# Small matmuls of the recurrence issued as groups with a higher rank, and modulation weights taken two blocks per step, in a two-layer hybrid backbone

## The chip, the cores and the metric

One core of one Trainium2 chip runs the whole program in a single launch. The metric is the device time of one execution in microseconds. The kernel before was run three times: 2420.04, 2423.49 and 2425.33 us, a median of 2423.49 us.

## The reference, cut to what matters

Two layers of one trunk run over 256 latent tokens and 256 context tokens of width 1024. A layer modulates a normalised input, projects it with one wide matrix into three token mixers, merges them, and then runs a feed-forward part: dense in layer 0, eight experts with two per token in layer 1.

```python
for i in range(DEPTH):
    mod = (silu_c @ w_mod[i] + b_mod[i])[:, None, :]      # 1024 -> 6144, for the latent row
    mod_c = silu_ctx @ w_mod[i] + b_mod[i]                # the same weights, for the context row
    ul = modulate(h, norm_mix[i], sh1, sc1) @ w_in[i]
    uc = modulate(hc, norm_mix[i], csh1, csc1) @ w_in[i]
    ...
def rwkv7_scan(S0, r, w, k, v, kk, a):                    # 8 heads, 2 directions, a 64x64 state
    S = S * w_t + (S @ -kk_t) (kk_t * a_t) + v_t k_t      # token by token
    y_t = S @ r_t
```

Two pieces of this are touched by the change. One is the modulation, a product of two vectors (latent and context) with a 1024x6144 matrix per layer. The other is the RWKV-7 recurrence, which the kernel computes in chunks of 64 tokens.

## The kernel before, in words

All operands are fp32. A large projection is done as three products of rounded halves (`mm3`, L917, L918 and L919): the weights arrive by DMA in a buffer `wraw`, ScalarE makes the rounded half `whi` (L893), VectorE makes the rest `wlo` (L895), and TensorE issues three matmuls of 128 rows by 128 columns of the array, mostly with 512 streamed columns. These are called large matmuls below. They use the array as one piece.

Four kinds of small matmuls use a part of the array, so that several can stand in it side by side:

- **Modulation** (`mods`, L1031). A block of 128 rows of the modulation matrix is streamed (128 columns, or 256 in the dense feed-forward stage of layer 0) against 32 columns of weights that hold the two vectors. Four such matmuls, one for each quarter `j` of the array's columns, belong to one block `k`; eight blocks are accumulated. `mods` is a generator that yields after each block. `fill` (MODF at L718) takes steps of it during the recurrence, `modnorm` (L1111) during the first norm, and `ffn` (L1470) two steps for each of 18 of its 22 column tiles, for the next layer.
- **Chunk products** (`rwkv_prod`, L389): 64 rows by 128 columns, 128 or 64 streamed columns; for each of four chunks one matmul for each of the two heads `h`, in two PSUM tiles `px`.
- **Inverse of a triangular block** (`rwkv_inverse`, L564, L573, L592, L602): 32 rows by 32 columns, 32 streamed columns; 32 matmuls (L564, L573) or 16 (L592, L602) in a row in the source.
- **Outputs of a chunk chain** (`rwkv_chain`, L658, L662): 128 rows by 64 columns.

The recurrence has eight units per layer (four head pairs, two directions). `rwkv_run` weaves the chain of one unit, the products and inverse of the next one, the elementwise part of the one after that, and `fill`, which supplies steps of the modulation and then of the large projections that other mixers need (`spills`). Weaving fixes only the order in which the source is traced. Each traced instruction gets a rank that counts up; when the program is built, a list scheduler keeps for each engine those instructions whose inputs and buffers its own model holds ready, and takes the one with the lowest rank. So each engine gets a fixed order of instructions before anything runs, and the hardware follows it.

PSUM has eight banks, dealt out by tag: the products use `aa` (two banks), the chain `ch` (one), the inverse `iv` (one), the outputs `oo` (one), modulation and spilled projections `fl` (two). `wraw` has four buffers.

Of the kernel before, what the change touches and what calls it, by code (L numbers as in the profile page):

```python
# [131 lines left out]
class Kern:  # L132
# [13 lines left out]


# [225 lines left out]
    def rwkv_prod(s, U):  # L373
# [7 lines left out]
        for half in range(2):  # L381
# [4 lines left out]
            for cc in range(4):  # L386
                c = half * 4 + cc
                for h, hr in enumerate(HRS):
                    nc.tensor.matmul(px[h][:, cc * 128:cc * 128 + N], U.BK[hr, c].rearrange("p a b -> p (a b)"), U.LA[hr, c].rearrange("p a b -> p (a b)")[:, 0:N], start=True, stop=True)  # L389
# [115 lines left out]
    def rwkv_inverse(s, Ac, FT):  # L505
# [55 lines left out]
        for u in range(8):  # L561
            for qd in range(4):
                qr = slice(qd * 32, qd * 32 + 32)
                nc.tensor.matmul(pq[qr, u * 32:u * 32 + 32], F16[qr, u, :], E[qr, u, :], start=True, stop=True)  # L564
# [5 lines left out]
        for u in range(8):  # L570
            for qd in range(4):
                qr = slice(qd * 32, qd * 32 + 32)
                nc.tensor.matmul(pe[qr, u * 32:u * 32 + 32], ET[qr, u, :], Q[qr, u, :], start=True, stop=True)  # L573
# [15 lines left out]
        for u in range(8):  # L589
            for h in range(2):  # L590
                a, b = slice(h * 64, h * 64 + 32), slice(h * 64 + 32, h * 64 + 64)
                nc.tensor.matmul(p2[b, u * 32:u * 32 + 32], FT[a, u, :], E2[a, u, :], start=True, stop=True)  # L592
# [6 lines left out]
        for u in range(8):  # L599
            for h in range(2):  # L600
                a, b = slice(h * 64, h * 64 + 32), slice(h * 64 + 32, h * 64 + 64)
                nc.tensor.matmul(pg[a, u * 32:u * 32 + 32], Q2[b, u, :], E2T[b, u, :], start=True, stop=True)  # L602
# [6 lines left out]
    def rwkv_chain(s, U):  # L609
# [12 lines left out]
        for k, c in enumerate(order):  # L622
# [27 lines left out]
            if c >= c0o and k % 4 == 3:  # L650

                po = s.tile(s.ps, [128, 512], "oo")
                g = c // 4
                for j in (g * 4, g * 4 + 2):
                    cb = j % 4 * 64
                    for odd, hr in enumerate(HRS):
                        if j + odd != order[0]:
                            mm(po[hr, cb:cb + 128], LA[:, j + odd, 1, :], S[:, order.index(j + odd) - 1], start=True, stop=False)  # L658
                    for h in range(2):
                        for odd, hr in enumerate(HRS):  # L660
                            first = j + odd == order[0]
                            mm(po[hr, cb + h * 64:cb + h * 64 + 64], MX[:, j + odd, h, 64:128], UV[:, j + odd, hs[h]], start=first, stop=first or h == 1)  # L662
# [55 lines left out]
MODF = [19, 10]  # L718
# [129 lines left out]
class Full(Kern):  # L848
# [162 lines left out]
    def mods(s, l):  # L1011
# [5 lines left out]
        for b in range(3):  # L1017
# [5 lines left out]
            for q in range(0, 4, n):  # L1023
                ps = s.tile(s.ps, [128, 512], s.mtag)
                for k in range(8):
                    if (b, q, k) in s.early:
                        wm = s.early.pop((b, q, k))
                    else:
                        wm = s.mod_block(l, b, q, k, s.wp, n)
                    for j in range(4):  # L1030
                        nc.tensor.matmul(ps[j * 32:j * 32 + 32, 0:n * 128].rearrange("p (q x) -> p q x", q=n), s.S[:, k, :], wm[:, :, j], start=k == 0, stop=k == 7)  # L1031
                    yield
# [70 lines left out]
    def modnorm(s, pool, gain, ish, isc, tts, mods=None):  # L1103
# [359 lines left out]
    def ffn(s, pool):  # L1463
# [5 lines left out]
        for f in range(22):  # L1469
            s.step(s.gen, 2 if f < 18 else 0)  # L1470
# [319 lines left out]
    def run(s, out):  # L1790
# [40 lines left out]
        s.step(s.gen, 4)  # L1831
# [112 lines left out]
```

## Time and profile before

| what | value |
|---|---|
| median of 3 runs | 2423.49 us |
| the profiled execution's own time | 2412.98 us |
| span of the profile, first to last instruction | 2411.2 us |
| mean granted TensorE clock, as a share | 0.97 |
| TensorE (PE) busy, and its matmul records | 2262.6 us, 15772 |
| weight loads (PEld) busy | 1785.6 us |
| VectorE (DVE) busy | 1538.5 us |
| ScalarE (ACT) busy | 1170.4 us |

A matmul on plain fp32 operands leaves two records in the trace, so a single small matmul reads as x2 and a group of 32 as x64; a large matmul leaves one. The start of a record is measured, its end is modelled. Matmuls overlap in the array, so what one costs is read from the distance between starts, not from its length. Some 1290 us of the span hold small matmuls of the four kinds above: the norm and recurrence of layer 0 (about 10 to 614 us), the dense feed-forward part (about 822 to 1135 us) and the norm and recurrence of layer 1 (about 1286 to 1659 us).

### The profile page before, as it was taken

To read this page: it belongs to the slowest core of one execution; us is meant where nothing else is said; L and a number is where in the kernel's file an instruction comes from. 1 tells how busy PE (TensorE), PEld (TensorE's weight loads), DVE (VectorE), ACT (ScalarE), POOL (GpSimd) and SP (SyncE) were. 2 spreads that over 40 slices of the span, in tenths; PEclk is the share of its full clock that TensorE was granted. 3 is DMA by queue.
4 is the path that set the end of the run, shared out by engine and by line. 5 is a ranking of instruction groups with operands and counts; after the bars stand their busy time and mean duration, and the time that the engine had idled before them with its cause. 6 is when DMAs were issued, how large, how long until landed. Compare 5 with 4: busy or idle time off the path is not lost. (4 is left out here: it accounts for less than half of the span.)

```text
span 2411.2 us, 41643 instructions
## 1 busy us (share of the span) xinstructions
PE 2262.6 (94%) x15772; PEld 1785.6 (74%) x15772; DVE 1538.5 (64%) x2994; ACT 1170.4 (49%) x2150; POOL 355.6 (15%) x307
## 2 busy tenths in 40 slices
PE   7989999999999989999998999999998989999996
PEld 4767777787667767778876777878867768878775
DVE  5776666655566453333227678777567578888897
ACT  4544444544543342222226554565363457777765
POOL 1311112101002210000013221130111211111120
PEclk9999999999999999999999999999899989999998
DMA  7343432223235424443223333322325658988895
GB/s 259 110 141 127 139 122 71 76 87 117 94 113 157 160 81 162 169 162 104 95 79 124 111 113 117 115 65 91 114 71 162 216 174 320 336 306 318 309 319 192
DMA packets 160609, 373.69 MB, mean 155 GB/s; under 512 B 18016, under 2 KB 35424, under 8 KB 160400
## 3 DMA queue, kind: packets, MB, share of 16 engines
q1 hardware_dynamic: 160400, 370.94, 45.9%
q8 instruction: 126, 2.06, 0.4%
q14 instruction: 83, 0.68, 0.1%
HBM read 345.18 MB, written 25.69 MB: 154 GB/s over the span
## 5 line engine op out<-in xcount | busy, mean ns | idle before, releaser
L895 DVE TENSOR_TENSOR wlo<-wraw,whi 128x512 fp32r<-128x512 f32 (+4 forms) x666 | 652.6, 1001 | 347.9 <-ACT whi L893 334.7
L893 ACT CAST whi<-wraw 128x512 fp32r<-128x512 f32 (+4 forms) x666 | 536.8, 820 | 557.2 <-PE mm L918 226.6
L917 PE MATMUL fl<-xh,whi 128*128 128x512 f32 (+1 forms) x816 | 317.0, 389 | 2.8 <-ACT whi L893 2.7
L919 PE MATMUL fl<-xh,wlo 128*128 128x512 f32 (+1 forms) x816 | 306.7, 376 | 6.7 <-DVE wlo L895 6.5
L918 PE MATMUL fl<-xl,whi 128*128 128x512 f32 (+1 forms) x816 | 302.4, 371 | 0.0
L919 PEld LDWEIGHTS fl<-xh,wlo 128*128 128x128 f32 x816 | 157.7, 193 | 31.6 <-DVE wlo L895 10.0
L917 PEld LDWEIGHTS fl<-xh,whi 128*128 128x128 f32 x816 | 158.0, 194 | 27.9 <-issue 6.0
L918 PEld LDWEIGHTS fl<-xl,whi 128*128 128x128 f32 x816 | 158.2, 194 | 21.3 <-issue 4.7
L917 PE MATMUL mm<-xh,whi 128*128 128x512 f32 (+1 forms) x416 | 165.6, 400 | 2.0 <-ACT pad L1797 1.0
L919 PE MATMUL mm<-xh,wlo 128*128 128x512 f32 (+1 forms) x416 | 162.5, 391 | 3.2 <-DVE wlo L895 3.1
L918 PE MATMUL mm<-xl,whi 128*128 128x512 f32 (+1 forms) x416 | 163.5, 393 | 0.0
L918 PE MATMUL mm<-wlo,xgh 128*128 128x512 f32 (+1 forms) x384 | 146.5, 381 | 15.3 <-DVE wlo L895 14.8
L917 PE MATMUL mm<-whi,xgh 128*128 128x512 f32 (+1 forms) x384 | 144.3, 378 | 0.2 <-ACT xs L1665 0.2
L919 PE MATMUL mm<-whi,xgl 128*128 128x512 f32 (+1 forms) x384 | 143.7, 374 | 0.0
L1696 POOL TENSOR_TENSOR H<-H,yt 128x512 f32<-128x512 f32 x29 | 56.1, 1960 | 392.5 <-DVE yt L1695 392.5
L918 PEld LDWEIGHTS mm<-wlo,xgh 128*128 128x128 f32 x384 | 72.2, 188 | 37.0 <-DVE wlo L895 27.0
L917 PEld LDWEIGHTS mm<-xh,whi 128*128 128x128 f32 x416 | 78.3, 189 | 27.3 <-ACT whi L893 4.9
L919 PEld LDWEIGHTS mm<-xh,wlo 128*128 128x128 f32 x416 | 78.4, 188 | 20.9 <-DVE wlo L895 4.9
L636 PEld LDWEIGHTS ch<-Pb,TT 128*128 128x128 f32 x512 | 71.8, 194 | 26.2 <-DVE Pb L630 17.3
L918 PEld LDWEIGHTS mm<-xl,whi 128*128 128x128 f32 x416 | 78.6, 189 | 16.3 <-DVE xl L711 0.8
L646 DVE SCALAR_TENSOR_TENSOR Sd<-ch,e2c,Se 64x64 f32<-64x64 f32 x192 | 53.8, 280 | 56.0 <-PE ch L641 53.4
L636 PE MATMUL ch<-Pb,TT 128*128 128x64 f32 x512 | 79.3, 278 | 8.9 <-DVE Pb L630 8.1
(527 smaller groups left out, 4688.1 us busy)
## 6 DMA issues: line engine op xcount, KB each, us to landing
wraw<-in_ws_dram SPq DMA_DIRECT2D x284, 512.0 KB
wraw<-in_ws_dram SPq DMA_DIRECT2D x302, 256.0 KB
wraw<-in_w_mod_dram SPq DMA_DIRECT2D x96, 256.0 KB
wraw<-in_ws_dram SPq DMA_DIRECT2D x64, 384.0 KB
wraw<-in_w_mod_dram SPq DMA_DIRECT2D x32, 512.0 KB
wm<-in_w_mod_dram SPq DMA_DIRECT2D x32, 256.0 KB
spg<-stg SPq DMA_DIRECT2D x24, 256.0 KB
mth<-spg SPq DMA_DIRECT2D x24, 256.0 KB
```

What stands on the lines that cost most here:

```text
L636: mm(ch[:, 128 + h * 64:192 + h * 64], U.TF[:, (2 * c + h) * 64:(2 * c + h) * 64 + 128], Pb[:, hs[h]], start=True, stop=True)
L646: nc.vector.scalar_tensor_tensor(S[hr, k, hr], ch[hr, o], e2c[hr, c, :], Se[hr, hr], ALU.mult, ALU.add)
L893: s.nc.scalar.copy(hi, raw)
L895: s.follow(s.nc.vector.tensor_sub(lo, raw, hi.bitcast(F32)))
L917: mm(out, ah, bh, start=start, stop=False)
L918: mm(out, ah, bl, start=False, stop=False)
L919: mm(out, al, bh, start=False, stop=stop)
L1696: eng.tensor_tensor(s.h[2 + i][:, ns], s.h[2 + i][:, ns], t, ALU.add)
```

## The change

A context `together` lowers the rank of each instruction traced inside it by 60, so that it competes with instructions that were traced 60 places earlier. It is put around the matmul loops of the chunk products, of the four steps of the inverse, of the chain's outputs, and of the modulation. In the modulation two blocks are taken per step, and the step counts are halved: MODF from 19 and 10 to 10 and 5, 3 and 5 steps in place of 5 and 9 in the first norm, one step for each of 20 column tiles in `ffn` in place of two for each of 18. The same matmuls, DMAs and vector instructions are issued as before, in another order.

```diff
+    def together(s):
+
+        return s.tc.high_priority(60)
...
             px = [s.tile(s.ps, [128, 512], "aa") for _ in HRS]
-            for cc in range(4):
-                c = half * 4 + cc
-                for h, hr in enumerate(HRS):
-                    nc.tensor.matmul(px[h][:, cc * 128:cc * 128 + N], ...
+            with s.together():
+                for cc in range(4):
+                    c = half * 4 + cc
+                    for h, hr in enumerate(HRS):
+                        nc.tensor.matmul(px[h][:, cc * 128:cc * 128 + N], ...
...
         pe = s.tile(s.ps, [128, 512], "iv")
-        for u in range(8):
-            for qd in range(4):
...
+        with s.together():
+            for u in range(8):
+                for qd in range(4):
...
-MODF = [19, 10]
+MODF = [10, 5]
...
-                for k in range(8):
-                    if (b, q, k) in s.early:
-                        wm = s.early.pop((b, q, k))
-                    else:
-                        wm = s.mod_block(l, b, q, k, s.wp, n)
-                    for j in range(4):
-                        nc.tensor.matmul(ps[j * 32:j * 32 + 32, ...], s.S[:, k, :], wm[:, :, j], start=k == 0, stop=k == 7)
+                for k in range(0, 8, 2):
+                    wm = [s.early.pop((b, q, kk)) if (b, q, kk) in s.early else s.mod_block(l, b, q, kk, s.wp, n) for kk in (k, k + 1)]
+                    with s.together():
+                        for kk, w in zip((k, k + 1), wm):
+                            for j in range(4):
+                                nc.tensor.matmul(ps[j * 32:j * 32 + 32, ...], s.S[:, kk, :], w[:, :, j], start=kk == 0, stop=kk == 7)
                     yield
...
-                s.step(mods, 9 if k else 5)
+                s.step(mods, 5 if k else 3)
...
-            s.step(s.gen, 2 if f < 18 else 0)
+            s.step(s.gen, 1 if f < 20 else 0)
...
-        s.step(s.gen, 4)
+        s.step(s.gen, 2)
```

The same wrapping is done for L564, L592 and L602 and for the output loop of `rwkv_chain`. In the changed program the line numbers are higher: L389 is L394, L573 is L580, L917 to L919 are L927 to L929, and L1031 is L1040.

Three places in TensorE's order show what moves. In the rows a name left of the arrow is the PSUM tile, right of it are the operands, and behind it stands the shape of the output.

In the dense feed-forward stage, TensorE's order before takes two modulation blocks (`aa`, 256 streamed columns) between two projections (`mm`):

```order
L917 MATMUL mm_9294<-xh_8582,whi_9297 128x512
L918 MATMUL mm_9294<-xl_8583,whi_9297 128x512
L919 MATMUL mm_9294<-xh_8582,wlo_9299 128x512
L1031 MATMUL aa_9152<-wraw_9328,S 32x256 x4
L1031 MATMUL aa_9152<-wraw_9334,S 32x256 x4
L917 MATMUL mm_9340<-xh_8582,whi_9343 128x512
L918 MATMUL mm_9340<-xl_8583,whi_9343 128x512
```

The same eight matmuls in the changed order:

```order
L1040 MATMUL aa_9152<-wraw_9328,S 32x256 x3
L927 MATMUL mm_9261<-xh_8582,whi_9264 128x512
L1040 MATMUL aa_9152<-wraw_9328,S 32x256
L928 MATMUL mm_9261<-xl_8583,whi_9264 128x512
L1040 MATMUL aa_9152<-wraw_9330,S 32x256
L929 MATMUL mm_9261<-xh_8582,wlo_9266 128x512
L1040 MATMUL aa_9152<-wraw_9330,S 32x256
L927 MATMUL mm_9261<-xh_8582,whi_9264 128x512
L1040 MATMUL aa_9152<-wraw_9330,S 32x256
L928 MATMUL mm_9261<-xl_8583,whi_9264 128x512
L1040 MATMUL aa_9152<-wraw_9330,S 32x256
L929 MATMUL mm_9261<-xh_8582,wlo_9266 128x512
```

The group now stands in the middle of the projection that was traced before it: three matmuls are left together, and five stand singly between large ones.

In the recurrence of layer 0, the second product of an inverse (`iv`, 32 matmuls) was cut once before, by a matmul of the chain (`ch`):

```order
L636 MATMUL ch_5635<-Pb_5675,TT_115_604 128x64 x2
L573 MATMUL iv_5692<-Q_5687,ET_5606 32x32 x13
L641 MATMUL ch_5635<-SU_613,BT_4811 128x128
L573 MATMUL iv_5692<-Q_5687,ET_5606 32x32 x19
L917 MATMUL fl_5610<-xh_205,whi_5729 128x512
```

and in the changed order, cut by the chain and by a spilled projection (`fl`):

```order
L580 MATMUL iv_5692<-Q_5687,ET_5606 32x32 x15
L645 MATMUL ch_5589<-Pb_5593,TT_115_604 128x64
L580 MATMUL iv_5692<-Q_5687,ET_5606 32x32
L645 MATMUL ch_5589<-Pb_5593,TT_115_604 128x64
L580 MATMUL iv_5692<-Q_5687,ET_5606 32x32 x11
L927 MATMUL fl_5610<-xh_205,whi_5613 128x512
L580 MATMUL iv_5692<-Q_5687,ET_5606 32x32
L928 MATMUL fl_5610<-xl_206,whi_5613 128x512
L580 MATMUL iv_5692<-Q_5687,ET_5606 32x32
L929 MATMUL fl_5610<-xh_205,wlo_5615 128x512
L580 MATMUL iv_5692<-Q_5687,ET_5606 32x32
L650 MATMUL ch_5589<-SU_613,BT_4811 128x128
```

It comes earlier against the chain (`ch_5589` is the chunk before `ch_5635`), and its second half is cut at nearly each matmul.

The chunk products (`aa`) of a unit of layer 0 stood as eight in a row before, the two heads in turn. In the changed order of TensorE the last four of them are cut by a projection:

```order
L927 MATMUL fl_924<-xh_205,whi_949 128x512
L394 MATMUL aa_1034<-LA_117_606,BK_986 128x128
L394 MATMUL aa_1035<-LA_117_606,BK_986 128x128
L394 MATMUL aa_1034<-LA_117_606,BK_986 128x128
L394 MATMUL aa_1035<-LA_117_606,BK_986 128x128
L928 MATMUL fl_924<-xl_206,whi_949 128x512
L394 MATMUL aa_1034<-LA_117_606,BK_986 128x128
L929 MATMUL fl_924<-xh_205,wlo_951 128x512
L394 MATMUL aa_1035<-LA_117_606,BK_986 128x128
L927 MATMUL fl_924<-xh_205,whi_949 128x512
L394 MATMUL aa_1034<-LA_117_606,BK_986 128x128
L928 MATMUL fl_924<-xl_206,whi_949 128x512
```

## Rows read from the trace of the kernel before

**Rows 1.** The profile's page: busy time, share of the span and instructions by engine.

```profile
PE 2262.6 (94%) x15772; PEld 1785.6 (74%) x15772; DVE 1538.5 (64%) x2994; ACT 1170.4 (49%) x2150; POOL 355.6 (15%) x307
```

**Rows 2.** Busy time by window; columns: window, length, engines' busy us, clock share, DMA.

```profile
10.00:614.00 604.00, 571.57 (x5243) 436.35 (x5244) 385.94 (x893) 276.53 (x599) 107.63 (x92) 0.98 0.38 122
822.00:1135.00 313.00, 306.22 (x1499) 236.88 (x1499) 111.52 (x176) 94.92 (x136) 8.08 (x6) 0.98 0.40 133
1286.00:1659.00 373.00, 352.25 (x3679) 288.18 (x3678) 274.03 (x626) 204.44 (x459) 85.23 (x77) 0.98 0.33 104
```

**Rows 3.** Waits of PE, 109 to 304 us: total us, times, longest.

```profile
PE iv L564 <- DVE E L558: 5.2, 2, 4.3
PE fl L1031 <- DMA wraw<-in_w_mod_dram: 1.3, 2, 0.9
```

**Rows 4.** Timeline of PE, a single modulation matmul; columns: start, length in us.

```profile
889.05 0.40 PE L919 MATMUL mm<-xh,wlo 128*128 128x512 f32 x1
889.29 0.65 PE L917 MATMUL mm<-xh,whi 128*128 128x512 f32 x2
889.86 0.62 PE L1031 MATMUL aa<-wraw,S 128*32 128x256 f32 x2
890.41 0.50 PE L918 MATMUL mm<-xl,whi 128*128 128x512 f32 x1
890.75 0.40 PE L919 MATMUL mm<-xh,wlo 128*128 128x512 f32 x1
```

**Rows 5.** Timeline of PE, eight such modulation matmuls in one group.

```profile
909.80 0.39 PE L919 MATMUL mm<-xh,wlo 128*128 128x512 f32 x1
910.12 1.07 PE L1031 MATMUL aa<-wraw,S 128*32 128x256 f32 x16
911.12 0.50 PE L917 MATMUL mm<-xh,whi 128*128 128x512 f32 x1
911.47 0.40 PE L918 MATMUL mm<-xl,whi 128*128 128x512 f32 x1
```

**Rows 6.** Timeline of PE, a single modulation matmul of 128 streamed columns.

```profile
1474.70 0.41 PE L1031 MATMUL fl<-wraw,S 128*32 128x128 f32 x2
1475.03 0.50 PE L919 MATMUL fl<-xh,wlo 128*128 128x512 f32 x1
1475.37 0.40 PE L917 MATMUL fl<-xh,whi 128*128 128x512 f32 x1
```

**Rows 7.** Timeline of PE, chunk products: a group of eight, and a single one.

```profile
100.59 1.16 PE L389 MATMUL aa<-LA,BK 64*128 64x128 f32 x16
...
380.43 0.48 PE L389 MATMUL aa<-LA,BK 64*128 64x128 f32 x2
380.85 0.49 PE L917 MATMUL fl<-xh,whi 128*128 128x512 f32 x1
```

**Rows 8.** Timeline of PE, inverse: a group of 32, and a single matmul.

```profile
137.11 0.75 PE L573 MATMUL iv<-Q,ET 32*32 32x32 f32 x64
137.80 0.50 PE L917 MATMUL fl<-xh,whi 128*128 128x512 f32 x1
...
254.49 0.24 PE L602 MATMUL iv<-F,Q 32*32 32x32 f32 x2
254.67 0.50 PE L917 MATMUL fl<-xh,whi 128*128 128x512 f32 x1
```

**Rows 9.** Timeline of weight loads at the single matmul of rows 4; last, idle time before.

```profile
889.86 0.14 PEld L1031 LDWEIGHTS aa<-wraw,S 128*32 128x32 f32 x2 [0.37 <-issue]
```

**Rows 10.** A window at half clock, and PE's timeline in it.

```profile
183.50:190.30 6.80, 6.80 (x84) 5.30 (x82) 3.72 (x9) 1.27 (x5) 0.96 (x1) 0.50 0.15 49
...
187.46 0.80 PE L919 MATMUL fl<-xh,wlo 128*128 128x512 f32 x1
188.05 0.63 PE L917 MATMUL fl<-xh,whi 128*128 128x512 f32 x1
```

More of the change, by code (lines that the diff above doesn't have):

```diff
@@ L560, in rwkv_inverse @@
         pq = s.tile(s.ps, [128, 512], "iv")
-        for u in range(8):
-            for qd in range(4):
-                qr = slice(qd * 32, qd * 32 + 32)
-                nc.tensor.matmul(pq[qr, u * 32:u * 32 + 32], F16[qr, u, :], E[qr, u, :], start=True, stop=True)
+        with s.together():
+            for u in range(8):
+                for qd in range(4):
+                    qr = slice(qd * 32, qd * 32 + 32)
+                    nc.tensor.matmul(pq[qr, u * 32:u * 32 + 32], F16[qr, u, :], E[qr, u, :], start=True, stop=True)
         yield
@@ L569, in rwkv_inverse @@
         pe = s.tile(s.ps, [128, 512], "iv")
[L570 to L573, printed above, removed]
+        with s.together():
+            for u in range(8):
+                for qd in range(4):
+                    qr = slice(qd * 32, qd * 32 + 32)
+                    nc.tensor.matmul(pe[qr, u * 32:u * 32 + 32], ET[qr, u, :], Q[qr, u, :], start=True, stop=True)
         yield
@@ L588, in rwkv_inverse @@
         p2 = s.tile(s.ps, [128, 512], "iv")
[L589 to L592, printed above, removed]
+        with s.together():
+            for u in range(8):
+                for h in range(2):
+                    a, b = slice(h * 64, h * 64 + 32), slice(h * 64 + 32, h * 64 + 64)
+                    nc.tensor.matmul(p2[b, u * 32:u * 32 + 32], FT[a, u, :], E2[a, u, :], start=True, stop=True)
         yield
@@ L598, in rwkv_inverse @@
         pg = s.tile(s.ps, [128, 512], "iv")
[L599 to L602, printed above, removed]
+        with s.together():
+            for u in range(8):
+                for h in range(2):
+                    a, b = slice(h * 64, h * 64 + 32), slice(h * 64 + 32, h * 64 + 64)
+                    nc.tensor.matmul(pg[a, u * 32:u * 32 + 32], Q2[b, u, :], E2T[b, u, :], start=True, stop=True)
         yield
@@ L653, in rwkv_chain @@
                 g = c // 4
[L654 to L659, printed above, removed]
-                        for odd, hr in enumerate(HRS):
-                            first = j + odd == order[0]
-                            mm(po[hr, cb + h * 64:cb + h * 64 + 64], MX[:, j + odd, h, 64:128], UV[:, j + odd, hs[h]], start=first, stop=first or h == 1)
+                with s.together():
+                    for j in (g * 4, g * 4 + 2):
+                        cb = j % 4 * 64
+                        for odd, hr in enumerate(HRS):
+                            if j + odd != order[0]:
+                                mm(po[hr, cb:cb + 128], LA[:, j + odd, 1, :], S[:, order.index(j + odd) - 1], start=True, stop=False)
+                        for h in range(2):
+                            for odd, hr in enumerate(HRS):
+                                first = j + odd == order[0]
+                                mm(po[hr, cb + h * 64:cb + h * 64 + 64], MX[:, j + odd, h, 64:128], UV[:, j + odd, hs[h]], start=first, stop=first or h == 1)
                 yield
@@ L1024, in mods @@
                 ps = s.tile(s.ps, [128, 512], s.mtag)
[L1025 to L1031 removed]
+                for k in range(0, 8, 2):
+                    wm = [s.early.pop((b, q, kk)) if (b, q, kk) in s.early else s.mod_block(l, b, q, kk, s.wp, n) for kk in (k, k + 1)]
+                    with s.together():
+                        for kk, w in zip((k, k + 1), wm):
+                            for j in range(4):
+                                nc.tensor.matmul(ps[j * 32:j * 32 + 32, 0:n * 128].rearrange("p (q x) -> p q x", q=n), s.S[:, kk, :], w[:, :, j], start=kk == 0, stop=kk == 7)
                     yield
```

2 lines of the change are left out of this document (1 added, 1 removed).

## The prediction

> **What bounds the kernel now.** I read the page's busy times first: TensorE is busy for 94% of the span and VectorE, the next, for 64% [rows 1]. Then I read the busy time in the three stretches that hold the small matmuls, because an average says nothing about them: of 604, 313 and 373 us TensorE is busy for 572, 306 and 352 us [rows 2]. So in all 1290 us that the change touches TensorE stands idle for about 60 us, and VectorE is busy for at most about three quarters. TensorE sets the pace there, and what lengthens its own stream lengthens the kernel. The waits come last: the longest kind in 109 to 304 us is the inverse waiting for VectorE, 5.2 us in two waits, and modulation waits for its DMA for 1.3 us [rows 3]. The stream is therefore the place to look, and the timeline shows what its members cost, from start to start.
>
> Large matmuls follow each other at 0.23 to 0.24 us: two in one row from 889.29 follow the one of 889.05 by 0.24 us [rows 4]. Around a small one this breaks. A single modulation matmul starts at 889.86, the next large one at 890.41, and the one after at 890.75 [rows 4]. Its weight load waited for 0.37 us though no engine held it ("issue") [rows 9]: whenever the part of the array in use changes, TensorE first lets the matmul in flight come to its end, and it cannot load the next weights under it. I call one stay in a small shape a visit. A visit has three parts: a late entry (909.80 to 910.12 is 0.32 us, against 0.23: 0.09), the time from the first small start to the next large start, and a late second large matmul (911.12 to 911.47 is 0.35, against 0.23: about 0.11) [rows 5]. So entry and return add 0.20 us to each visit, whatever is done in it.
>
> **What the change does to the visits.** The two orders can be counted before anything runs. Before, TensorE changes the shape in use 737 times; after, 1500 times. The group's rank is lowered by 60, but the large matmuls traced up to 60 places earlier hold those very ranks and are still waiting, so the scheduler takes them in turn: one small, one large. Instead of a group moved ahead as one, the order has a group riveted into a projection. Visits go from 116 to 279 for modulation (97 more with 128 streamed columns, 66 more with 256, in the dense feed-forward part), from 55 to 144 for chunk products (89 more), from 113 to 231 for the inverse (118 more), and 13 more for the outputs: 383 more.
>
> **Their price.** Prices for a visit of a single matmul, first small start to next large start plus the 0.20 us:
>
> - modulation, 256 columns: 890.41 less 889.86 is 0.55, so 0.75 [rows 4]; 66 of them make 49.5 us;
> - modulation, 128 columns: 1475.03 less 1474.70 is 0.33, so 0.53, and the second large one is late there as well, 0.34 us [rows 6]; 97 make 51.4 us;
> - chunk products: 380.85 less 380.43 is 0.42, so 0.62 [rows 7]; 89 make 55.2 us;
> - inverse: 254.67 less 254.49 is 0.18, so 0.38 [rows 8]; 118 make 44.8 us;
> - outputs have no row of their own here; I take the modulation's 0.53, and 13 make 6.9 us.
>
> That is 208 us. Against it stands the room that singled matmuls leave in their groups. 395 more matmuls stand alone after than before. In a group one more modulation matmul costs little: eight with 256 columns take 1.00 us, one takes 0.55, so 0.064 each [rows 4, 5], and half of that with 128 columns; a chunk product costs (1.16 - 0.48)/7, or 0.10 us [rows 7]; one of the inverse (0.69 - 0.18)/31, or 0.016 us [rows 8]. With 70, 106, 87 and 132 of them that is 4.5, 3.4, 8.4 and 2.1 us, some 18 us. TensorE's stream grows by **190 us**.
>
> The Trainium skill ("TensorE: Matmul & The Clock Gate", section "Single matmul latency") puts the part of a matmul's latency that a stream hides at about 166 ns at full clock; by it, an estimate, the 763 added changes of shape (1500 less 737), one exposed latency each, would be 127 us. The rows above give more because a visit of one matmul also loses its neighbours in the other quarters of the array.
>
> **What takes from it and adds to it.** The 60 us in which TensorE stands idle are waits for others. Those engines issue the same instructions, so a wait shrinks where TensorE arrives later; none of them shrinks where the late visit is itself the cause, as in a chain that goes from TensorE to VectorE and back. The ends are 0 and 60 us; I take 30. A new wait could come from fetching two blocks per step: a pair holds two of the four `wraw` buffers. The DMA order on SP keeps its pattern of two blocks and two weight tiles in the feed-forward part, DMA is busy for 0.40 of the time there [rows 2], and modulation's wait for DMA was 1.3 us [rows 3]; I take 0, and 5 us if each of some 15 steps there waited a third of a microsecond. The halved step counts cover the same blocks and cost nothing by themselves: they are covered by the projections around them, and if a step came late, the norm of the next layer would wait for it. The granted clock fell to one half where small visits were dense: 0.50 (1.2 GHz of 2.4) in 183.5 to 190.3 us, and the large matmul after a visit took 0.59 us there in place of 0.34 [rows 10]. I take 5 us, between 0 and the rival below.
>
> The sum: 190 - 30 + 5 = 165 us. The profiled execution took 2412.98 us, so 2578; the median of the three runs is 10.5 us above that execution, so the forecast for a median is **2588 us**. Without the waits' shrinking, and with a quarter of the clock rival's 105 us, it would be about 2640; with all 60 us hidden and the single visits a fifth cheaper, 2412.98 + 190 - 60 - 38 is 2505, or 2515 as a median.
>
> **The rivals.**
>
> *The clock gives way.* The 395 single matmuls, with the large ones between them, fill some 300 us (0.75 us each). If the clock is halved in half of that, a visit there costs 1.7 times as much (0.59/0.34) [rows 10], 105 us more: about 2690. For it: the clock did fall in such a place. Against it: it came back within 6.8 us with the same mix running, and over the three stretches it is granted at 0.98 [rows 2]. The Trainium skill ("TensorE: Matmul & The Clock Gate", section "A second HAM failure mode: psum-queue depth-cycling") tells of a kernel whose clock went back and forth between its two levels among its groups of matmuls; no run here yet shows it for this order.
>
> *The visits hide behind other work.* If all the 60 us of waits go and half the price of a visit falls where TensorE would soon have waited anyway, 95 - 60 leaves 35 us: 2458. Against it: in the feed-forward stretch TensorE waits for 7 of 313 us [rows 2], and the prices there are a quarter of the sum.
>
> *Faster: groups stay whole.* If the hardware ran each group in one piece, visits would fall to the number of groups: 80, 32, 64 and 24 in place of 116, 55, 113 and 59. At 0.53, 0.62, 0.38 and 0.53 us that saves 19 + 14 + 19 + 19, some 71 us: 2353. It decides where the count of visits falls below the 737/2 of before. Against it: the order built has twice as many, and the trace of before has TensorE's matmuls in the order that its program lists.
>
> *No change.* It needs the whole 190 us to be covered, and TensorE has 60 us of cover.
>
> **How the numbers follow.** The forecast, visits paid nearly in full, has 0.80 and runs from 2505 to 2665 us: the low end is the sum with all cover used and cheaper visits, the high end the sum with no cover and some of the clock rival. The clock rival beyond that has 0.08, the hidden visits 0.05, whole groups 0.04, no change 0.03. A measurement of this kernel tells 0.2% (about 5 us) from no change. So slower by more than that has 0.80 + 0.08 + 0.05 = 0.93, within it 0.03, faster 0.04.
>
> **What would show it.** In the profile after: about 15772 matmul records as before; TensorE's busy share stays at 94% or rises; the feed-forward stretch grows by some 40 us with one small and one large matmul in turn, a large one every 0.98 us (0.55 + 0.43) there; the two recurrences grow by some 90 and 30 us; the expert part after 1940 us keeps its length. A single visit is again 0.55, 0.33, 0.42 and 0.18 us from start to start. I am wrong if the visits in the trace are not doubled, if single visits are much cheaper in the new order, or if TensorE's waits grow instead of shrinking; a clock below 0.94 over a stretch would speak for the first rival.

## The result, and the profile after

The changed kernel takes 2742.83 us (median of 4 runs, 2710.94 to 2763.65) against 2421.76 us: a ratio of 1.127, with a 95% interval of 1.120 to 1.133. That ratio is taken from the runs counted as fast, without the one of 2763.65 us; the two medians by themselves give 1.133. The forecast was 2588 us with a range up to 2665. The sign was right, the size was not. The profiled execution took 2744.19 us, its span is 2742.3 us against 2411.2 before, 331 us more, and its mean granted clock is 0.917 against 0.97.

The page of the kernel after, busy times and the row of the granted clock in 40 slices (in tenths of full speed); they answer to [rows 1]. The last line is the clock row of the kernel before:

```profile
PE 2575.7 (94%) x15772; PEld 1910.4 (70%) x15772; DVE 1552.5 (57%) x2994; ACT 1168.3 (43%) x2150; POOL 358.0 (13%) x307
...
PEclk9957986977999998899999999999999898999998
...
PEclk9999999999999999999999999999899989999998
```

The number of records is the same, TensorE's share too, and the other engines do the same work. TensorE's busy time has grown by 313 us, and the time in which it is not busy by 18 (from 148.6 to 166.6). The clock row says where: it reads 5 to 8 in most of slices 3 to 10, some 140 to 690 us, which is the recurrence of layer 0. The row of the kernel before has no digit below 9 there.

Windows of the kernel after that hold the same large matmuls as the windows of before in the next fence; columns as in [rows 2] (length, then the busy times of TensorE, its weight loads, VectorE, ScalarE and GpSimd, the clock, and DMA share and rate):

```profile
137.30:688.80 551.50, 525.87 (x3692) 347.06 (x3690) 247.79 (x562) 166.53 (x379) 62.22 (x49) 0.76 0.23 75
142.90:200.90 58.00, 54.69 (x313) 27.44 (x313) 9.20 (x14) 10.54 (x24) 0.53 (x1) 0.50 0.18 57
1154.50:1415.20 260.70, 260.70 (x1101) 179.18 (x1100) 72.12 (x87) 59.20 (x75) 0.00 (x0) 1.00 0.36 124
1656.30:1867.30 211.00, 199.25 (x1719) 141.95 (x1718) 121.78 (x294) 84.41 (x197) 34.57 (x29) 0.94 0.27 88
2292.00:2742.30 450.30, 414.72 (x1953) 340.04 (x1951) 391.08 (x399) 319.70 (x402) 60.01 (x32) 0.98 0.83 298
```

The same of the kernel before (the window at 142.9 us has no partner):

```profile
120.00:486.70 366.70, 344.67 (x3695) 267.14 (x3692) 243.60 (x573) 167.69 (x379) 62.95 (x50) 0.97 0.35 112
924.80:1145.60 220.80, 220.80 (x1101) 173.53 (x1100) 70.78 (x87) 58.95 (x74) 0.00 (x0) 1.00 0.45 150
1378.00:1550.20 172.20, 164.21 (x1804) 130.80 (x1801) 126.05 (x311) 90.42 (x211) 33.49 (x30) 0.98 0.34 108
1960.60:2411.20 450.60, 414.81 (x1953) 340.06 (x1951) 390.13 (x399) 319.83 (x402) 59.98 (x32) 0.98 0.84 298
```

Read them in pairs. The experts are unchanged. The feed-forward stretch is 39.9 us longer with a clock of 1.00 and no idle time in either kernel: this is the price of visits, alone. The recurrence of layer 0 is 184.8 us longer, and its clock went from 0.97 to 0.76. That of layer 1 is 38.8 us longer, with a clock of 0.94; its window after holds 85 records of small matmuls fewer than the one before, so 38.8 is a little too low.

The timeline of TensorE in the feed-forward stretch after; it answers to [rows 4]:

```profile
1180.34 0.49 PE L927 MATMUL mm<-xh,whi 128*128 128x512 f32 x1
1180.77 0.62 PE L1040 MATMUL aa<-wraw,S 128*32 128x256 f32 x2
1181.31 0.49 PE L928 MATMUL mm<-xl,whi 128*128 128x512 f32 x1
```

One large and one small matmul stand in turn, and a large one starts every 0.97 us.

The timeline of TensorE in the recurrence of layer 0, kernel after; in the brackets is the idle time before the row, and what ended it:

```profile
146.21 0.65 PE L570 MATMUL iv<-E,F 32*32 32x32 f32 x32 [6.00 <-DVE E L563]
146.79 0.80 PE L929 MATMUL fl<-xh,wlo 128*128 128x512 f32 x1
...
148.70 0.31 PE L570 MATMUL iv<-E,F 32*32 32x32 f32 x2
148.94 0.80 PE L928 MATMUL fl<-xl,whi 128*128 128x512 f32 x1
...
172.93 0.79 PE L394 MATMUL aa<-LA,BK 64*128 64x128 f32 x2
173.65 0.79 PE L929 MATMUL fl<-xh,wlo 128*128 128x512 f32 x1
...
178.13 0.64 PE L1040 MATMUL fl<-wraw,S 128*32 128x128 f32 x2
```

TensorE waits 6.00 us for the operand `E` of an inverse. From 142.9 us, inside this wait, the granted clock is 0.50 (1.2 GHz), and it stays there for 58 us, while single matmuls of the inverse, of the products and then of the modulation stand between large ones. The kernel before has the same wait at the same place:

```profile
131.97 0.93 PE L564 MATMUL iv<-E,F 32*32 32x32 f32 x64 [4.34 <-DVE E L558]
132.82 0.80 PE L917 MATMUL fl<-xh,whi 128*128 128x512 f32 x1
...
135.12 0.63 PE L919 MATMUL fl<-xh,wlo 128*128 128x512 f32 x1
...
135.86 0.39 PE L918 MATMUL fl<-xl,whi 128*128 128x512 f32 x1
```

There the clock fell as well, but behind the wait came one whole group and then only large matmuls. The fall lasted 3.4 us; from 135.86 us on the large matmuls are back at their length of 0.39 us.

By the trace's record of the clock, the window of layer 0 has four such falls before, of 3.4 to 6.8 us each, and nine after, five of them 31 to 58 us long. Not each begins with a wait. Two windows of the kernel after, around the fall at 641.3 us:

```profile
631.10:641.30 10.20, 10.20 (x74) 7.04 (x73) 8.34 (x14) 4.12 (x9) 0.00 (x0) 1.00 0.16 51
641.30:672.00 30.70, 30.70 (x238) 20.56 (x237) 4.78 (x12) 6.58 (x18) 0.00 (x0) 0.50 0.08 27
```

TensorE is busy for all of the 10.2 us ahead of this fall, the last 3.5 of them with single matmuls of the inverse between large and chain matmuls. What stands in the five long falls can be counted in the trace, a stay being an unbroken row of matmuls of one small kind: 151 stays of the inverse, 29 of the products, 9 of the outputs, and 16 of the modulation, all 16 in the first fall.

Three of TensorE's waits in the kernel after, whole program (us in total, times, longest), and the first two as they were before:

```profile
PE ch L634 <- DVE Sd L655: 16.8, 12, 4.2
...
PE iv L570 <- DVE E L563: 12.8, 4, 6.0
...
PE aa L394 <- POOL BK L369: 4.7, 1, 4.7
```

```profile
PE iv L564 <- DVE E L558: 9.1, 4, 4.3
PE ch L625 <- DVE Sd L646: 8.9, 15, 2.9
```

### The profile page after: what moved, and what is told of

Its sections match the earlier page's. It is cut to its first block, busy times and chain, and to the rows that moved or that the text cites. A ratio compares the mean times of both kernels' runs of the same rounds, so it can differ in the third digit from the quotient of the medians.

```text
span 2742.3 us, 41611 instructions
## 1 busy us (share of the span) xinstructions
PE 2575.7 (94%) x15772; PEld 1910.4 (70%) x15772; DVE 1552.5 (57%) x2994; ACT 1168.3 (43%) x2150; POOL 358.0 (13%) x307
## 5 line engine op out<-in xcount | busy, mean ns | idle before, releaser
L927 PE MATMUL fl<-xh,whi 128*128 128x512 f32 (+1 forms) x816 | 345.7, 424 | 2.0 <-ACT whi L903 2.0
L929 PE MATMUL fl<-xh,wlo 128*128 128x512 f32 (+1 forms) x816 | 333.3, 409 | 4.0 <-DVE wlo L905 3.9
L928 PE MATMUL fl<-xl,whi 128*128 128x512 f32 (+1 forms) x816 | 331.6, 406 | 0.0
L929 PEld LDWEIGHTS fl<-xh,wlo 128*128 128x128 f32 x816 | 164.9, 202 | 38.3 <-issue 10.9
L927 PEld LDWEIGHTS fl<-xh,whi 128*128 128x128 f32 x816 | 165.3, 203 | 35.8 <-issue 16.5
L928 PEld LDWEIGHTS fl<-xl,whi 128*128 128x128 f32 x816 | 165.6, 203 | 29.0 <-issue 13.0
L929 PE MATMUL mm<-xh,wlo 128*128 128x512 f32 (+1 forms) x416 | 166.9, 401 | 3.2 <-DVE wlo L905 3.2
L927 PE MATMUL mm<-xh,whi 128*128 128x512 f32 (+1 forms) x416 | 168.2, 406 | 1.7 <-ACT pad L1806 1.0
L927 PE MATMUL mm<-whi,xgh 128*128 128x512 f32 (+1 forms) x384 | 144.2, 378 | 0.2 <-ACT xs L1674 0.2
L929 PE MATMUL mm<-whi,xgl 128*128 128x512 f32 (+1 forms) x384 | 143.7, 374 | 0.0
L401 DVE TENSOR_TENSOR MX<-aa,consts 128x512 f32<-128x512 f32 (+1 forms) x64 | 39.6, 623 | 127.4 <-ACT AF L400 115.6
L394 PE MATMUL aa<-LA,BK 64*128 64x128 f32 (+1 forms) x512 | 96.8, 334 | 6.6 <-POOL BK L369 4.7
L929 PEld LDWEIGHTS mm<-xh,wlo 128*128 128x128 f32 x416 | 79.2, 190 | 31.8 <-DVE wlo L905 8.6
L927 PEld LDWEIGHTS mm<-xh,whi 128*128 128x128 f32 x416 | 79.1, 191 | 31.7 <-issue 12.5
L645 PEld LDWEIGHTS ch<-Pb,TT 128*128 128x128 f32 x512 | 79.4, 210 | 28.2 <-DVE Pb L639 18.3
```

The costliest lines, as they stand in the source:

```text
L401: nc.vector.tensor_mul(MX[:, cs, h, 0:N], pv[:, :, 0:N], bc(mk[:, 0:N], 4, 1))
L645: mm(ch[:, 128 + h * 64:192 + h * 64], U.TF[:, (2 * c + h) * 64:(2 * c + h) * 64 + 128], Pb[:, hs[h]], start=True, stop=True)
L927: mm(out, ah, bh, start=start, stop=False)
L928: mm(out, ah, bl, start=False, stop=False)
L929: mm(out, al, bh, start=False, stop=stop)
```

## The experiments

Theory A is a fixed price per visit, as predicted. Theory B is that groups are taken before their inputs are ready. Theory C is the clock. To lay them beside each other, the growth of each span over the 2411.2 us of before is cut into three parts. **Stream**: each visit in the run's own order, at the prices of the prediction. **Not busy**: the span less TensorE's busy time, against 148.6 us. **Clock**: the granted clock has two levels, so the time at half clock is twice the missing share of the mean clock times the span (145 us before, 455 after; the 110 and 113 us that some expectations name for before are too low), and what was added costs 0.42 us for each, a rate that the ninth run gave by itself.

| run | changes of shape | stream | not busy | half clock added, cost | sum | span grew by |
|---|---|---|---|---|---|---|
| the whole change | 1500 | +180 | +18 | 310, +130 | +328 | +331 |
| e1, two blocks only | 675 | -14 | +6 | 10, +4 | -4 | +2 |
| e2, rank 1000 | 731 | +1 | +25 | 18, +7 | +33 | +50 |
| e3, rank modulation only | 1092 | +100 | +4 | 54, +23 | +127 | +133 |
| e4, rank recurrence only | 1275 | +105 | +9 | 284, +119 | +233 | +233 |
| e5, rank inverse only | 926 | +29 | +10 | 110, +46 | +85 | +88 |
| e6, rank products only | 833 | +29 | +10 | 69, +29 | +68 | +73 |
| e7, inverse at 1000 | 655 | -17 | +13 | 30, +12 | +8 | +13 |
| e8, modulation at 1000 | 704 | -13 | +20 | 41, +17 | +24 | +36 |
| e10, rank 200 | 742 | +5 | +26 | 84, +35 | +66 | +80 |
| e12, two blocks again | 675 | -14 | +6 | 25, +10 | +2 | +8 |
| e11, rank 20 | 1847 | +245 | -1 | 538, +226 | +470 | +456 |

Each row is a single execution, the profiled one, laid against a single execution of before, which was among the fastest. In 54 further executions on four chips the kernel before had a clock of 0.959 to 0.974, which is 125 to 200 us at half clock. So an entry below some 55 us in the column of the clock is within the spread of the kernel before. The same spread confirms the rate: two executions of before with spans of 2410.5 us (clock 0.973) and 2439.6 us (0.959) differ by 29 us and by 70 us at half clock, or 0.42; two of the whole change, 2709.1 us (0.930) and 2742.3 us (0.917), differ by 33 and 76 us, or 0.44.

Times below are medians against a kernel before that ran on the same chip (2417.72 to 2426.29 us).

**e1: two blocks per step, no rank.**

```diff
     def together(s):
-        return s.tc.high_priority(60)
+        return ExitStack()
```

> Two blocks per step and the halved step counts stay; no matmul gets a changed rank. Counted in TensorE's order: 675 changes of shape (737 before, 1500 after the whole change); visits of modulation 107 (116), of the inverse 87 (113). Theory A, the visits are the whole cost and two blocks per step cost nothing: the stream shrinks by some 14 us by the prices of the prediction, so 2400 to 2420 us. Theory B, a pair of blocks holds two of four weight buffers and delays the projections: 2430 us or more. Theory C, the halved clock: no more half-clock time than before (about 113 us of the span).

2418.71 us, a ratio of 0.9973 (0.9935 to 1.0011). The halved step count is not what cost the time. One wait has grown without any lowered rank, that of the chain for `Sd` (8.9 us before); the row of e1:

```profile
PE ch L634 <- DVE Sd L655: 13.8, 21, 2.8
```

The same kernel was run again, for twelve executions:

> The kernel of the first experiment again (two blocks per step, no rank lowered), with more rounds, since its ratio of 0.9973 could not be told from no change. Its order has 675 changes of shape in place of 737; by the prices of the rows the stream is 14 us shorter. Theory A: 2421 - 14 = 2407 us, a ratio of 0.994. Theory B, what the stream gives is lost again in waits and in half clock, as in the run with whole groups of the inverse (17 us shorter, ratio 0.9996): 0.998 to 1.002.

2411.74 us, a ratio of 0.9978 (0.9960 to 0.9996). It may be faster by 0.2%, just what can be told from no change, and it is the only version whose interval lies below the kernel before.

**e2: rank lowered by 1000.**

```diff
-        return s.tc.high_priority(60)
+        return s.tc.high_priority(1000)
```

> The whole change with 1000 places in place of 60: groups should be issued in one piece. Counted: 731 changes of shape, visits of modulation 123, products 68, inverse 70, outputs 67; single matmuls in visits about as before. Theory A (visits): stream +1 us, so 2410 to 2430 us if nothing else matters. Theory B (rank itself, small matmuls taken so early that chain and projections come late): clearly over 2440 us with more waits of TensorE. Theory C (clock): half-clock time near that of before, about 110 us.

2476.1 us, 1.020 (1.014 to 1.026). The shape changes as often as before, and yet it is slower: TensorE is not busy for 25 us more. Its waits, kernel of e2:

```profile
PE aa L394 <- DVE BK L365: 11.2, 4, 5.7
...
PE aa L394 <- POOL BK L369: 6.9, 3, 4.7
PE aa L1040 <- DMA wraw<-in_w_mod_dram: 5.6, 11, 2.2
```

Groups of products stand ahead of their operand `BK`, those of the modulation ahead of their weights. That is theory B, for about half of the 50 us by which the span grew.

**e3: only the modulation's rank lowered by 60; e4: only the recurrence's.** The edit of e4; in e3 the two helpers change places:

```diff
+    def together_mod(s):
+
+        return ExitStack()
+
...
-                    with s.together():
+                    with s.together_mod():
                         for kk, w in zip((k, k + 1), wm):
```

> 60 places and two blocks for the modulation alone; the recurrence's four groups keep their rank. Counted: 1092 changes of shape, visits of modulation 328 (more than the 279 after the whole change), inverse 167, products 79. Stream by the prices: +100 us, of which some 45 in the dense feed-forward part. Theory A (fixed price per visit): 2520 us. Theory C (the clock falls where single visits follow each other in the recurrence, and doubles what they cost there): half-clock time clearly over 113 us, and 2560 to 2610 us; the feed-forward part stays at full clock and grows by the 40 to 46 us of the price list.

> 60 places for products, inverse and outputs alone; modulation takes two blocks per step at its own rank. Counted: 1275 changes of shape, visits of the inverse 276, products 146, outputs 74, modulation 113. Stream by the prices: +105 us, nothing of it in the feed-forward part. Theory A: 2527 us. Theory C: half-clock time of some 200 to 300 us in the two recurrences, and 2580 to 2640 us. The feed-forward part keeps its length of before.

e3 took 2531.04 us, 1.042 (1.036 to 1.048), e4 2655.31 us, 1.094 (1.088 to 1.101). Their stretches (layer 0's recurrence, then the feed-forward part), first e3, then e4:

```profile
123.80:535.90 412.10, 391.43 (x3696) 281.68 (x3693) 245.08 (x573) 167.39 (x379) 62.80 (x50) 0.95 0.32 100
988.00:1248.60 260.60, 260.60 (x1101) 179.17 (x1100) 72.09 (x87) 59.11 (x75) 0.00 (x0) 1.00 0.36 124
```

```profile
133.70:672.20 538.50, 516.33 (x3692) 349.01 (x3691) 249.13 (x562) 166.25 (x379) 62.00 (x49) 0.77 0.24 77
1119.70:1340.00 220.30, 220.30 (x1102) 173.72 (x1101) 70.91 (x87) 58.96 (x74) 0.00 (x0) 1.00 0.46 150
```

Both have a stream that is some 100 us longer. In e3 that is nearly all: the feed-forward part takes its 39.8 us, and the recurrence keeps a clock of 0.95. (The profiled execution, at 0.961 over the whole span, was the slowest of five; the others have 0.969 or 0.970, as before.) In e4 the clock of the recurrence is 0.77, as in the whole change, and costs more than the visits; its time lies above the 2640 us that theory C allowed. So theory A holds for the modulation, and the clock is brought down by the groups of the recurrence.

**e5 and e6: the inverse alone, the products alone.** From here on the helper takes a number, which is 0 at all loops but those named:

```diff
-    def together(s):
+    def together(s, n):
 
-        return s.tc.high_priority(60)
+        return s.tc.high_priority(n) if n else ExitStack()
...
-        with s.together():
+        with s.together(60):
             for u in range(8):
                 for qd in range(4):
```

> The whole change, but the rank is lowered (by 60) only for the four matmul loops of the inverse. Its order has 926 changes of shape (before 737, the whole change 1500), 200 visits of the inverse (113 before), 114 of them single. Theory A, each visit at the price of the rows and nothing else: the stream grows by 29 us, so about 2455 us. Theory C, the clock falls where single matmuls of the inverse stand between large ones: the run with all recurrence groups ranked had 283 us more at half clock; if the inverse brings it, 200 us or more at half clock are added and 0.42 us is lost for each, so about 2535 to 2570 us, with a mean clock of 0.93 to 0.94. Theory B, groups come before their inputs are ready: a new wait of TensorE for VectorE in the inverse, 10 us or more.

> The whole change, but the rank is lowered (by 60) only for the chunk products. Its order has 833 changes of shape, 136 visits of products (55 before), 93 of them single. Theory A, each visit at the price of the rows and nothing else: the stream grows by 28.5 us, so about 2455 us. Theory C with the products as the cause of the fallen clock: 200 us or more added at half clock, so about 2535 to 2570 us; with the inverse as the cause, this run stays near 2455 with a clock of 0.96 to 0.97. If neither kind alone brings the clock down, it takes both together. Theory B: new waits for the products' operands BK and LA, 10 us or more.

2498.96 us, 1.032 (1.028 to 1.035), and 2492.78 us, 1.031 (1.027 to 1.035). Both miss both expectations: each is between the price of its visits (2455) and a clock that gives way in full. The inverse adds 110 us at half clock. The products add 69 in the profiled execution, and 69 or 110 in the other three (clocks of 0.949 and 0.957). Together, with the outputs, they added 284 in e4. So neither kind alone brings the whole of it.

**e7 and e8: the inverse, and the modulation, lowered by 1000.** For e7, and likewise at the modulation's loop for e8:

```diff
-        with s.together(60):
+        with s.together(1000):
             for u in range(8):
                 for qd in range(4):
```

> The whole change, but the rank is lowered only for the inverse, and by 1000, past everything that waits beside it. In its order each of the 64 groups of the inverse stands in one piece (64 visits, none single; before 113), 655 changes of shape. Theory A: the stream shrinks by 17 us against the kernel before, so 2404 to 2412 us, a ratio of 0.991 to 0.995. Theory B, a group taken so early makes other engines' work come in a worse order: what the stream gives is lost in waits, 2420 to 2450 us. Theory C adds that the clock is no lower than before (half clock 150 us or less).

> The whole change, but the rank is lowered only for the modulation, and by 1000. Its order has 704 changes of shape, 119 visits of the modulation, none single; by the prices of the rows the stream shrinks by 13 us. All groups ranked by 1000 gave 2476 us, 50 us more than before, with a stream as long as before. Theory B1, the modulation's groups are taken before their weights have landed: this run repeats most of that, 2450 to 2475 us, with waits of TensorE for DMA wraw<-in_w_mod of 5 us or more. Theory B2, the 50 us come from the recurrence's groups: this run is at 2405 to 2420 us.

e7 took 2421.12 us, 0.9996 (0.9979 to 1.0014): with all 64 groups of the inverse whole, 17 us of stream are saved and given back, 13 us of them in waits; the 12 us that the table puts down to the clock are within the spread of the kernel before. e8 took 2458.65 us, 1.018 (1.013 to 1.022), with 6.1 us of waits for `wraw` by DMA in the feed-forward part; that is B1 by its time. A group that stays whole is worth something only if its inputs are there when its turn comes.

**e9: the alternation by itself.** A program of its own, executed once:

```python
for f in kinds:              # none, mod 256, mod 128, inverse, product, inverse and product in turn
    for i in range(80): large(xh)
    for i in range(120): f(i); large(xh)
    ...                      # VectorE and ScalarE make a new xh from the last PSUM tile
    for i in range(120): f(i); large(xh)
```

> A program of its own that computes nothing of the reference: only matmuls of one large and one single small kind in turn, on loaded inputs. For each of six cases (large alone; modulation with 256 and with 128 streamed columns; inverse; products; inverse and products in turn) it issues 80 large matmuls, 120 pairs of a single small and a large matmul, lets TensorE wait some 6 us for a chain on VectorE, and issues 120 such pairs again. Theory A, prices of the rows at full clock: a pair every 0.98 us (256 columns), 0.76 (128 columns), 0.85 (products), 0.61 (inverse), large alone 0.23. Theory C1, a wait brings the clock down and single matmuls of some kinds keep it down: the 120 pairs before the wait are granted 1.0 in all cases; after the wait the clock is 0.5 and stays there for 40 us or more with the inverse, the products and both in turn, and comes back within some 15 us with modulation and with large matmuls alone. Theory C2, the mix alone brings the clock down: the 120 pairs of the inverse or of the products lose the clock before the wait too. If all cases behave alike, the kinds of matmul do not matter, and what holds the clock down in the recurrence is something else (the waits in it, or its share of tiny matmuls).

Windows of e9: large alone after the wait; then modulation with 256 and with 128 columns, each before and after the wait; the inverse, its first 6.3 us and the rest before the wait; products before and after it; and, in the last line, inverse and products in turn before the wait and up to its end:

```profile
58.10:86.90 28.80, 28.80 (x121) 23.71 (x122) 0.39 (x2) 0.00 (x0) 0.00 (x0) 0.95 0.00 1
105.70:221.90 116.20, 116.20 (x359) 38.73 (x358) 0.00 (x0) 0.00 (x0) 0.00 (x0) 1.00 0.00 0
226.30:358.20 131.90, 131.89 (x360) 42.09 (x361) 0.43 (x2) 0.00 (x0) 0.00 (x0) 0.86 0.00 0
376.80:467.70 90.90, 90.90 (x359) 38.72 (x358) 0.00 (x0) 0.00 (x0) 0.00 (x0) 1.00 0.00 1
472.10:626.20 154.10, 154.10 (x361) 56.64 (x362) 0.38 (x2) 0.00 (x0) 0.00 (x0) 0.50 0.00 0
645.40:651.70 6.30, 6.30 (x33) 3.37 (x31) 0.00 (x0) 0.00 (x0) 0.00 (x0) 1.00 0.00 0
651.70:757.30 105.60, 105.60 (x328) 50.75 (x327) 0.00 (x0) 0.00 (x0) 0.00 (x0) 0.50 0.00 0
897.50:998.30 100.80, 100.80 (x359) 57.47 (x358) 0.00 (x0) 0.00 (x0) 0.00 (x0) 1.00 0.00 0
1002.70:1175.40 172.70, 172.70 (x360) 94.03 (x361) 0.38 (x2) 0.00 (x0) 0.00 (x0) 0.50 0.00 0
1195.00:1337.10 142.10, 137.76 (x359) 71.65 (x358) 4.03 (x10) 0.30 (x1) 0.00 (x0) 0.53 0.00 0
```

And the timeline of TensorE at the wait ahead of 472.1 us, then products at full and at half clock:

```profile
472.07 0.79 PE L38 MATMUL big<-whi,xh 128*128 128x512 f32 x1 [4.34 <-ACT xh L74]
...
900.42 0.49 PE L46 MATMUL small<-C,x 64*128 64x128 f32 x2
900.84 0.50 PE L38 MATMUL big<-whi,xh 128*128 128x512 f32 x1
901.27 0.49 PE L46 MATMUL small<-C,x 64*128 64x128 f32 x2
...
1010.63 0.79 PE L46 MATMUL small<-C,x 64*128 64x128 f32 x2
1011.35 0.79 PE L38 MATMUL big<-whi,xh 128*128 128x512 f32 x1
```

Theory A's prices hold: at full clock a pair takes 0.97 us (116.2/120), 0.76 and 0.84, and the inverse 0.61 from start to start (expected 0.98, 0.76, 0.85, 0.61). Of the clock theories each has a part:

- Modulation and products keep 1.00 for over 90 us before the wait. After some 4.3 us of waiting the clock is 0.50, and with 128 columns and with products it does not come back in 154 and 173 us. With 256 columns it comes back after some 37 us (2 x 0.14 x 131.9), with large matmuls alone after 3. This is C1, except that the modulation with 128 columns was expected to recover.
- The inverse loses the clock without any wait, some 6 us into the alternation, and does not regain it while the alternation lasts. Inverse and products in turn do the same after some 10 us. This is C2.

The operands get new values at each wait, but the large matmuls that open the next case use these values too, and there the clock was back at 1.00 within some 3 us each time.

A pair of products takes 1.44 us at half clock (172.7/120) in place of 0.84, so each microsecond there costs 0.60/1.44 = 0.42 us; with modulation of 128 columns it is (1.28 - 0.76)/1.28 = 0.41. That is the rate in the table.

**e10 and e11: the rank lowered by 200, and by 20.** For e10, with 20 for e11:

```diff
-        return s.tc.high_priority(60)
+        return s.tc.high_priority(200)
```

> The whole change with a rank lowered by 200 in place of 60. Its order has 742 changes of shape (before 737, with 60 1500, with 1000 731): 123 visits of modulation, 75 of products, 71 of the inverse, 68 of the outputs; by the prices of the rows the stream is 5 us longer than before. Theory A: 2421 + 5 = 2426 us, within 10. Theory B, groups taken before their inputs are ready cost waits, less of them than with 1000 (50 us): 2440 to 2465 us. Theory C: half clock stays under 190 us.

> The whole change with a rank lowered by 20 in place of 60. Its order has 1847 changes of shape: 299 visits of modulation, 145 of products, 374 of the inverse (247 single), 128 of the outputs; by the prices of the rows the stream is 245 us longer than before. Theory A without the clock: 2666 us. Theory C: the recurrences have more single matmuls of the inverse than with 60 (458 us at half clock there), so 450 us or more at half clock, 0.42 us lost for each of the 300 added: about 2795 us, and a mean clock of 0.91 or less.

e10 took 2481.95 us, 1.022 (1.017 to 1.027), slower than any theory gave. `BK` is waited for 11.2 us as in e2, half clock grew to 229 us, and some 14 us stay unexplained. e11 took 2872.5 us against 2423.38. Theory C gave 2795: 538 us at half clock were added, not 300, and at 0.42 each the sum of the table comes to 470 us where the span grew by 456. Windows of e11 with the recurrences of layer 0 and of layer 1:

```profile
125.40:699.00 573.60, 552.22 (x3691) 359.27 (x3690) 244.27 (x568) 168.28 (x381) 63.29 (x49) 0.76 0.22 72
1708.80:1972.50 263.70, 255.96 (x1822) 176.90 (x1819) 119.51 (x301) 89.82 (x210) 32.78 (x29) 0.71 0.22 70
```

Layer 0 has the clock of the whole change, 0.76. In layer 1, where the whole change still had 0.94, e11 has 0.71.

## Why the prediction was wrong in size, point by point

- **TensorE's stream bounds the touched stretches: right.** It is busy for 94% as before, and the busy times of VectorE, ScalarE and GpSimd are within 1%.
- **The visits, doubled: right.** The trace shows the counts of the built order: 279 visits of modulation for 116 before, 231 of the inverse for 113. e1 takes the rank out, and the whole loss goes with it.
- **The price of a visit: right.** The prediction's sum of means gave 190 us, the same prices laid on the built order visit by visit give 180. The feed-forward stretch grew by 39.9 us where some 40 were forecast (its own price list adds up to 45: 66 visits at 0.75 us, less 4.5), with a large matmul every 0.97 us where 0.98 was. The Trainium skill ("TensorE: Matmul & The Clock Gate", section "Single matmul latency") puts the constant part of a bf16 matmul's latency at 166 ns at full clock; an estimate from it, one such latency for each of 132 more changes of shape, would be 22 us for that stretch. The measured 39.9 us decide against it.
- **Waits shrink by 30 us: wrong in sign.** The time in which TensorE is not busy grew by 18 us. The prediction reasoned that TensorE would arrive later and find its inputs ready. But its queue is a fixed order: a group moved ahead 60 places meets its operand earlier, not later, and the engine stands in front of it (6.00 us at 146.21, 4.34 before). The runs bear this out for the operands of the moved groups: the waits for `E` (9.1 us before, 12.8 after) are 11.5 us in e4 and 13.5 in e5, which move the inverse, and 6.4, 6.6 and 3.8 us in e1, e3 and e6, which do not. It is not the reason for the longer wait of the chain for `Sd` (8.9 us before, 16.8 after), which is 13.8 us in e1 already, where no rank is lowered. Some 6 of the 18 us come with e1; what lengthens the wait for `Sd` was not tried.
- **The clock, 5 us: this is the step that failed.** It cost about 130 us in the profiled execution (310 us more at half clock, at 0.42), and about 100 in the one with a clock of 0.930. Of the 166 us by which the span grew beyond the 165 forecast, it makes some 125, the waits 48 (18 more in place of 30 fewer), and the visits take 10 off. The first rival, "the clock gives way", is what happened. Its 105 us were near, and its chance of 0.08 was far too small. The prediction dismissed it because in 183.5 to 190.3 us the clock came back "with the same mix running" [rows 10]. It was not the same mix: in before, a fallen clock meets whole groups and runs of large matmuls, among which it was back after 3.4 us at 135 us. The mean of 0.98 over the stretches said only that nothing there held the clock down yet. In the new order there are few such runs. Of some 600 large matmuls in the windows of layer 0, 451 stood in runs of six or more before and 161 after; 5 stood alone before and 160 after. Single matmuls, most of them of the inverse, stand between them, and the fall at 142.9 us lasts 58 us. The prediction had named both signs of this: waits that grow, and a clock below 0.94 over a stretch.
- **The shares by stretch: right, once the clock is taken out.** In the layer 0 recurrence 184.8 us were added; its windows have 265 and 22 us at half clock, so 243 x 0.42 = 102 of them are the clock, and 83 are left, where some 90 were forecast. In that of layer 1, 38.8 less 8 leaves 31, where 30 were.
- **No cost of two blocks per step: right.** e1 and its repetition are at or just below the kernel before.

Shown by runs are the price of the visits, that the recurrence's groups bring the clock down (e4 against e1 and e3), and that an alternation of small and large matmuls can hold it down (e9). Which kind does so in the kernel is read from the trace. The long falls of the whole change are full of single matmuls of the inverse, and in e5, which moves the inverse alone, the two longest falls in layer 0 are 37.5 us each, with 30 and 32 stays of the inverse and none of another small kind. The modulation adds no half clock that can be told from the spread: e4, where its rank is not lowered, has 284 to 323 us more in its four executions, the whole change 235 to 316 in three. The falls begin in more than one way. Of the nine in layer 0, seven come inside a wait of TensorE or within 3 us behind one; two, at 521.8 and 641.3 us, have no wait in the 8 us ahead of them, but single matmuls of the products or of the inverse in turn with large ones. Whether it is the kind of the small matmul or the lack of runs of large ones that keeps the clock down was not separated.

A version with groups that stay whole and never stand ahead of their inputs was not found: e7 and e8 gave back what their stream saved, and e2 and e10, with a stream about as long as before, lost time in waits.

## What to carry to other kernels

Lowering a group's rank by a fixed distance keeps the group together only if nothing else that is ready holds the ranks in between; count the changes of shape in the built order before believing that a group is one. When an engine's stream is stretched by such changes, price them from single visits in the trace, and then ask separately whether the new order still has runs of large matmuls in which a fallen clock can come back. A mean clock near 1 says that it does now, not that it will.

## What was not expected of the hardware

**TensorE at half clock without idle time.** In e9 TensorE is busy for 154.1 of 154.1 us by the profile and is granted 0.50 throughout. The Trainium skill ("TensorE: Matmul & The Clock Gate", section "What's actually happening") says that the clock follows how busy the array has lately been. This trace does not agree, if busy means what the profile counts: one small and one large matmul in turn fill the row and do not bring the clock back.

**The same mix has two states.** Products in turn with large matmuls ran 100.8 us at 1.00 and, after one wait of 4.34 us, 172.7 us at 0.50 for another 120 such pairs. Only the cases with the inverse, the smallest matmul here, lost the clock without a wait.
